# Where the taps of a depthwise convolution stand in VectorE's queue: behind each other, or one behind every eleventh matmul

## The chip, the cores and the metric

The kernel runs on one core of a Trainium2 chip. The metric is the device time of one execution in microseconds (us). The median of three runs of the kernel before is 1765.89 us (1764.24 to 1766.59). For this kernel, differences under about 0.2% (3.5 us) can't be told from no change.

## The reference, cut to what matters

One layer of a decoder trunk on 1024 tokens of 1024 channels. Three branches read the same normalized input and are merged by gates; a SwiGLU layer follows. The change touches branch B, the convolution module:

```python
a, ag = jnp.split(conv_in, 2, axis=-1)          # 512 channels each, from xn @ w_in
u = a * jax.nn.sigmoid(ag)
u = jnp.pad(u, ((0, 0), (30, 0), (0, 0)))
u = lax.conv_general_dilated(u, conv_w, (1,), 'VALID', ...,
                             feature_group_count=512) + conv_b   # depthwise, 31 taps, causal
u = jax.nn.silu(layer_norm(u, conv_ln_g, conv_ln_b))             # over the 512 channels
br_conv = u @ w_conv_out
```

Branch A is native sparse attention (compressed blocks, selected blocks, sliding window), branch C is cross-attention of 4 heads into 256 memory tokens. Everything is float32.

## The kernel before, in words

Every float32 product of two operands is made of three matmuls on halves that were split into a high and a low part (`mm3`, line 143, each through `mm`, line 140 and 141). The split is a copy on ScalarE (line 130) and a subtraction on VectorE or GpSimd (line 127, from `sub`).

The order of the instructions on each engine is not written by hand. The program is traced in the order of the source, and a planner then lays the instructions out when the program is built: it keeps a planned time for each engine and, where several instructions are ready, takes the one with the best priority, which is that of the source order. `with low(n)` makes the priority of what stands in it worse by n. What is in such a block is taken when nothing else is ready for the engine. On the chip each engine then runs its queue strictly in the planned order and waits at semaphores.

Two kinds of work have such a low priority. The **taps** (lines 356 to 361) are 31 VectorE instructions for each of four channel tiles `ct`, so 124: one `tensor_scalar` (line 358) and 30 `scalar_tensor_tensor` of about 1000 columns (line 360). The **fill** (lines 753 to 766) are 24 units of merge-gate projections into the bank `pf`, of which the first 12 (`N_EARLY`) may run whenever TensorE has nothing else; each unit is 48 matmuls of 512 columns, written out through ScalarE (`fz`, line 765).

The order of the source around the change is: memory query projection of two heads (`QMQ[0]`, 192 matmuls of `mm`), then for each `ct` the two GLU projections (96 matmuls of 512 columns for a `ct`, 24 for each of two halves and two weights) and the taps; the branch gates (32); the projections of the compressed keys and values (`compress_in`, 96) and their small network (`compress`, 36, with transposes and a VectorE copy at line 419 in between); the memory keys and values (`tok_proj`, 192); `mem_attention` twice (288 each: in four steps `tp`, 12 for scores, 48 of a projection, 12 for values); the last query projection `Q[1]` (192 in all). Then follows the layer norm of the convolution (lines 556 to 584): sums over the four channel tiles on GpSimd (`sum4`, line 560), a mean by a matmul with ones, squares, sums again, root, reciprocal, products, silu, and the store to `ud`. After it come the key and value projections KS, VS, KW, VW (lines 587 to 611) and the sparse attention.

A pool of 16 slabs holds the large tiles (`N_MAIN`): 8 of the normalized input, 4 of the convolution (`U`: input and accumulator of each `ct`, free after the store to `ud`), 2 of the queries, and others such as KS, VS, KW, VW.

The taps of the kernel before are traced inside the loop over `ct`, straight behind the GLU products of their own tile, and the planner lays each of them where VectorE has no other ready work.

Of the kernel before, what the change touches and what calls it, by code (L numbers as in the profile page):

```python
# [12 lines left out]
OP = mybir.AluOpType  # L13
# [5 lines left out]
S = 1024  # L19
# [10 lines left out]
TAPS = 31  # L30
FILL, TAP = 2000000, 1000000
ORDER = mybir.DependencyInfo(mybir.DependencyClass.NoSync, mybir.DependencyReason.DATA)
# [6 lines left out]
def hybrid_layer_kernel(  # L39
# [4 lines left out]
    nc = tc.nc  # L44
# [25 lines left out]
    def slab(shape, dt=F32R):  # L70
        return slabs.tile([P] + shape, dt, tag="slab", name=nm("slab"))
# [16 lines left out]
    def t2(shape, dt=F32, p=P):  # L88
        return t2p.tile([p] + shape, dt, tag="t2", name=nm("t2"))
# [8 lines left out]
    def bank(shape, dt=F32, p=P, at=None):  # L98
        if at is None:
            turn[1] += 1  # L100
            at = order[turn[1] % len(order)]
        return psp[at].tile([p] + shape, dt, tag=f"ps{at}", name=nm("ps"))
# [9 lines left out]
    def const(shape, dt, name, p=P):  # L112
        return cp.tile([p] + shape, dt, tag=name, name=name)
# [19 lines left out]
    def recip_rms(ss, n, eps, w):  # L133
# [3 lines left out]
        nc.vector.reciprocal(q, r)  # L137
        return q

    def mm(o, a, b, start, stop):  # L140
        return nc.tensor.matmul(o, a, b, start=start, stop=stop)  # L141

    def mm3(o, ah, al, bh, bl, start, stop):
        first = mm(o, ah, bh, start, False)
        mm(o, ah, bl, False, False)
        mm(o, al, bh, False, stop)
        return first
# [27 lines left out]
    cw = const([4, TAPS + 3], F32, "cw")  # L175
# [72 lines left out]
    def col_unit(w, c0, n=P, alloc=wslab, eng=None, load=False):  # L248
        return unit(w[:, c0:c0 + n].rearrange("(k p) c -> p k c", p=P), [w.shape[0] // P, n], alloc, eng,
                    load)  # L250
# [5 lines left out]
    def chan_proj(w, half, act=xn, n=P, alloc=bank):  # L256
        o = alloc([512])
        for k in range(KT):
            mm3(o[:n], w[:, 0, k, :], w[:, 1, k, :], act(0, k, half), act(1, k, half), k == 0, k == KT - 1)
        return o  # L260
# [28 lines left out]
    def head_norms(raw, gain):  # L289

        h, d = raw.shape[2:]
        ss = small(NT * h)
        for tp in range(4):
            sq = t2([2, h, d])
            nc.scalar.activation(sq, raw[:, 2 * tp:2 * tp + 2], AF.Square)
            nc.vector.tensor_reduce(ss[:, 2 * tp * h:2 * (tp + 1) * h], sq.rearrange("p a h d -> p (a h) d"),
                                    axis=AX.X, op=OP.add)
        r = recip_rms(ss, d, RMS_EPS, NT * h).rearrange("p (a h) -> p a h", a=NT)
        for tp in range(4):
            v = raw[:, 2 * tp:2 * tp + 2]  # L300
            nc.vector.tensor_tensor(v, v, r[:, 2 * tp:2 * tp + 2, :, None].to_broadcast([P, 2, h, d]), op=OP.mult)
            if gain is not None:
                gain_mul(v, gain)
# [27 lines left out]
    b = bank([4, TAPS + 3])  # L331
# [5 lines left out]
    b = bank([2, 16])  # L337
# [3 lines left out]
    nc.sync.dma_start(w2s, cmp_w2[0].rearrange("s (j p) d -> p s j d", p=P))  # L341


    U = []
    for ct in range(4):
        wag = col_unit(w_in, C_AG + ct * P)
        wa = col_unit(w_in, C_A + ct * P)
        uc = slab([2, S], F32)
        U.append(uc)
        for half in range(2):  # L350
            pg = chan_proj(wag, half)
            sg = t2([512])
            nc.scalar.activation(sg, pg, AF.Sigmoid)
            pa = chan_proj(wa, half)
            nc.vector.tensor_tensor(uc[:, 0, half * 512:(half + 1) * 512], pa, sg, op=OP.mult)
        with low(TAP):
            u, acc = uc[:, 0], uc[:, 1]
            nc.vector.tensor_scalar(acc, u, cw[:, ct, 30:31], cw[:, ct, 31:32], op0=OP.mult, op1=OP.add)
            for s in range(1, TAPS):
                nc.vector.scalar_tensor_tensor(acc[:, s:], u[:, :S - s], cw[:, ct, 30 - s:31 - s], acc[:, s:],  # L360
                                               op0=OP.mult, op1=OP.add)


    st = stage.tile([P, KT, 24], F32, tag="st", name=nm("st"))
# [14 lines left out]
    b = bank([NT, 24])  # L379
# [78 lines left out]
    for hp in range(2):  # L458
# [4 lines left out]
        b = bank([2, 256])  # L463
# [88 lines left out]
        raw_proj(ws, tp, Q[1])  # L552
    head_norms(Q[1], None)


    def sum4(part):
        for a, b_ in ((0, 1), (2, 3), (0, 2)):
            i0 = U[a][:, part] if (a, b_) != (0, 2) else U[0][:, 0]
            i1 = U[b_][:, part] if (a, b_) != (0, 2) else U[2][:, 0]
            nc.gpsimd.tensor_tensor(U[a][:, 0], i0, i1, op=OP.add)  # L560

    sum4(1)
    for half in range(2):
        c = slice(half * 512, (half + 1) * 512)
        pm_ = bank([512])
        mm(pm_, ones, U[0][:, 0, c], True, True)
        for ct in range(4):
            nc.vector.tensor_tensor(U[ct][:, 1, c], U[ct][:, 1, c], pm_, op=OP.subtract)
    for ct in range(4):
# [183 lines left out]
    with low(FILL):  # L753
        for n_ in range(3 * KT):
            b_, d_ = n_ // KT, n_ % KT
            w = col_unit(w_in, C_GM + b_ * D + d_ * P, alloc=fslab, eng=nc.gpsimd)
            for h_ in range(2):
                ps = fbank([512])
                for k in range(KT):
                    first = mm3(ps, w[:, 0, k, :], w[:, 1, k, :], xn(0, k, h_), xn(1, k, h_), k == 0, k == KT - 1)  # L760
                    j = ((n_ - N_EARLY) * 2 + h_) * KT + k
# [7 lines left out]
    acc = [slab([2, S], F32) for _ in range(4)]  # L769
# [3 lines left out]
    for n_, (br, src, wt) in enumerate(branches):  # L773
        ins = nxt
        for dp in range(4):
# [3 lines left out]
            for d_ in (2 * dp, 2 * dp + 1):  # L779
# [4 lines left out]
                for half in range(2):  # L784
# [7 lines left out]
                    a = acc[dp][:, d_ % 2, half * 512:(half + 1) * 512]  # L792
# [5 lines left out]
                    if n_ == 2:  # L798
                        if d_ % 2 == 0:
                            MG[half][dp] = slab([2, 2, 512])  # L800
                        m = MG[half][dp]
# [327 lines left out]
```

## Time and profile before

| | us |
|---|---|
| median of three runs | 1765.89 |
| lowest and highest run | 1764.24, 1766.59 |
| the profiled execution, whole | 1765.17 |
| its span, first to last instruction | 1763.4 |
| TensorE matmul busy in it | 1706.7 (97%) |
| VectorE busy in it | 1071.1 (61%) |
| ScalarE busy in it | 724.7 (41%) |
| GpSimd busy in it | 664.4 (38%) |

The trace calls the engines PE (TensorE matmul), PEld (its weight loads), DVE (VectorE), ACT (ScalarE), POOL (GpSimd) and SP (the queue of the transfers). In the tables of stretches a row begins with the stretch and its length; then each engine has its busy time in us and, in brackets, the number of its instructions that lie in the stretch; then come PEclk, the mean busy share of the transfer engines and what they moved in GB/s. PEclk is the granted clock of TensorE as a share of 2.4 GHz, so that 0.50 is the lower of its two levels, 1.2 GHz. In a timeline one row is a run of instructions of one kind, with its start, its length, the number merged into it, and in square brackets the idle time of the engine ahead of it and what ended that.

### The profile page before, as it was taken

To read this page: it belongs to the slowest core of one execution; us is meant where nothing else is said; L and a number is where in the kernel's file an instruction comes from. 1 tells how busy PE (TensorE), PEld (TensorE's weight loads), DVE (VectorE), ACT (ScalarE), POOL (GpSimd) and SP (SyncE) were. 2 spreads that over 40 slices of the span, in tenths; PEclk is the share of its full clock that TensorE was granted. 3 is DMA by queue.
4 is the path that set the end of the run, shared out by engine and by line. 5 is a ranking of instruction groups with operands and counts; after the bars stand their busy time and mean duration, and the time that the engine had idled before them with its cause. 6 is when DMAs were issued, how large, how long until landed. Compare 5 with 4: busy or idle time off the path is not lost.

```text
span 1763.4 us, 25092 instructions
## 1 busy us (share of the span) xinstructions
PE 1706.7 (97%) x9431; PEld 1482.2 (84%) x9431; DVE 1071.1 (61%) x1794; ACT 724.7 (41%) x1355; POOL 664.4 (38%) x543
## 2 busy tenths in 40 slices
PE   7999779999999999999999999989999999999999
PEld 6887669899988888989888899868888888888887
DVE  5599994435445667767755623596454554457655
ACT  6212224344455666766654423333222222234332
POOL 1113458333343434434203500456656767510000
PEclk9999899999999999999999999989999999999999
DMA  6113314211122111111286323123233444794673
GB/s 220 48 27 114 126 42 132 78 55 39 65 66 64 49 37 49 37 34 46 86 300 202 121 73 120 72 72 120 90 107 117 140 156 157 245 394 166 213 242 124
DMA packets 178527, 204.59 MB, mean 116 GB/s; under 512 B 10788, under 2 KB 125764, under 8 KB 177382
## 3 DMA queue, kind: packets, MB, share of 16 engines
q1 hardware_dynamic: 178406, 202.99, 35.2%
q8 instruction: 74, 1.21, 0.3%
q14 instruction: 47, 0.39, 0.1%
HBM read 152.62 MB, written 50.33 MB: 115 GB/s over the span
## 4 chain that ended last, share of the span: by engine, by line
PE 84%; DVE 10%; POOL 2%; ACT 1%; DMA 1%; issue 1%; SPq 0%; DVEq 0%; ACTq 0%; POOLq 0%
PE ps L141 51%; PE pf L141 16%; PE ps L1064 11%; DVE slab L360 6%; PE ps L714 3%; PE pf L1064 1%; DVE slab L127 1%; POOL wsl L127 1%; DVE t L127 1%; POOL t L127 1%; PE ps L208 1%; DMA slab<-in_x_dram 1%; DMA fst<-in_w_in_dram 0%; PE ps L640 0%; PE ps L515 0%
## 5 line engine op out<-in xcount | busy, mean ns | idle before, releaser
L141 PE MATMUL ps<-slab,wsl 128*128 128x512 f32 x1596 | 370.9, 390 | 0.3 <-ACT wsl L130 0.3
L141 PEld LDWEIGHTS ps<-slab,wsl 128*128 128x128 f32 x1596 | 299.0, 188 | 63.1 <-ACT wsl L130 0.8
L141 PE MATMUL pf<-slab,fsl 128*128 128x512 f32 x1260 | 327.8, 399 | 4.5 <-ACT fz L765 1.8
L141 PEld LDWEIGHTS pf<-slab,fsl 128*128 128x128 f32 x1260 | 226.6, 188 | 46.8 <-ACT fz L765 3.6
L141 PE MATMUL ps<-wsl,slab 128*128 128x256 f32 x1744 | 235.7, 291 | 12.9 <-POOL wsl L127 8.1
L141 PEld LDWEIGHTS ps<-wsl,slab 128*128 128x128 f32 x1744 | 225.3, 198 | 16.7 <-POOL wsl L127 8.5
L360 DVE SCALAR_TENSOR_TENSOR slab<-slab,cw 128x1007 f32<-128x1007 f32 (+27 forms) x120 | 174.5, 1501 | 0.4
L954 DVE TENSOR_TENSOR t<-ps,t 128x512 f32<-128x512 f32 x124 | 85.0, 688 | 109.2 <-PE ps L141 104.4
L127 DVE TENSOR_TENSOR t<-ps,t 128x512 fp32r<-128x512 f32 (+2 forms) x192 | 117.5, 630 | 44.6 <-ACT t L130 43.1
L141 PE MATMUL ps<-slab,fsl 128*128 128x512 f32 x612 | 142.1, 389 | 0.0
L141 PEld LDWEIGHTS ps<-slab,fsl 128*128 128x128 f32 x612 | 114.9, 188 | 23.9
L1064 PE MATMUL ps<-wsl 128*128 128x512 f32 x504 | 120.6, 389 | 0.0
L127 POOL TENSOR_TENSOR wsl<-st,wsl 128x1024 fp32r<-128x1024 f32 x20 | 72.9, 3659 | 122.9 <-ACT wsl L130 110.4
L141 PE MATMUL ps<-t,slab 128*128 128x256 f32 x624 | 115.6, 292 | 2.6 <-DVE t L127 2.1
L130 ACT CAST t<-ps 128x512 fp32r<-128x512 f32 (+2 forms) x192 | 97.9, 540 | 42.1 <-PE ps L714 30.5
L130 ACT CAST wsl<-st 128x1024 fp32r<-128x1024 f32 x66 | 69.3, 1050 | 110.5 <-PE ps L141 66.4
L1064 PEld LDWEIGHTS ps<-wsl 128*128 128x128 f32 x504 | 94.6, 188 | 19.6
L141 PEld LDWEIGHTS ps<-t,slab 128*128 128x128 f32 x624 | 93.9, 189 | 9.5 <-DVE t L127 3.0
L141 PE MATMUL ps<-slab,qt 128*128 128x384 f32 (+3 forms) x384 | 96.2, 342 | 0.5 <-DVE sm L682 0.5
L127 POOL TENSOR_TENSOR fsl<-fst,fsl 128x1024 fp32r<-128x1024 f32 x24 | 62.7, 2614 | 81.2 <-ACT fsl L130 81.2
L127 DVE TENSOR_TENSOR wsl<-st,wsl 128x1024 fp32r<-128x1024 f32 x46 | 62.3, 1355 | 49.9 <-ACT wsl L130 49.8
L628 POOL TENSOR_SCALAR wsl<-wsl,sm 128x640 f32<-128x640 f32 (+7 forms) x76 | 52.7, 707 | 91.2 <-DVE sm L626 53.4
(238 smaller groups left out, 2772.5 us busy)
## 6 DMA issues: line engine op xcount, KB each, us to landing
t<-in_w_down_dram SPq DMA_DIRECT2D x70, 256.0 KB, 3.8
fst<-in_w_in_dram SPq DMA_DIRECT2D x24, 512.0 KB, 3.9
zd<-fz SPq DMA_DIRECT2D x48, 256.0 KB, 2.0
t<-zd SPq DMA_DIRECT2D x24, 512.0 KB, 3.5
st<-in_w_in_dram SPq DMA_DIRECT2D x22, 512.0 KB, 3.9
st<-in_w_gate_dram SPq DMA_DIRECT2D x22, 512.0 KB, 4.0
st<-in_w_up_dram SPq DMA_DIRECT2D x22, 512.0 KB, 4.4
ad<-t SPq DMA_DIRECT2D x44, 256.0 KB, 2.4
```

The costliest lines, as they stand in the source:

```text
L127: eng.tensor_tensor(o, a, b, op=OP.subtract)
L130: nc.scalar.copy(hi, src)
L141: return nc.tensor.matmul(o, a, b, start=start, stop=stop)
L208: nc.tensor.transpose(b[:, kk, tt * P:(tt + 1) * P], js[tt][:, k * P:(k + 1) * P], ident)
L360: nc.vector.scalar_tensor_tensor(acc[:, s:], u[:, :S - s], cw[:, ct, 30 - s:31 - s], acc[:, s:], op0=OP.mult, op1=OP.add)
L628: nc.gpsimd.tensor_scalar(tiles[h], tiles[h], c[:, h:h + 1], 1.0, op0=OP.mult, op1=OP.mult)
L714: nc.tensor.transpose(b[:, j - j0, h, :], tiles[h][:, j * P:(j + 1) * P], ident)
L954: nc.vector.tensor_tensor(o, a_, b_, op=OP.add)
L1064: nc.tensor.matmul(B[t], a_, b_, start=start and k == 0 and j == 0, stop=k == FH - 1 and j == 2, skip_group_check=True)
```

## The change

A list `products` takes down every matmul that goes through `mm`, in the order of the source. The taps are no longer traced in the loop over `ct`: the loop only notes them, in the same order, and the place in `products` where the first tile's GLU products end. All 124 taps are traced after `head_norms(Q[1], None)`, ahead of the layer norm, with the same low priority as before. Tap `j` gets a manual dependency on one product: the products from the first place to the end of the `Q[1]` projection are divided into 128 equal parts, and tap `j` stands behind the first product of part `j`. The dependency is of the class `NoSync`: it holds for the planner's order and puts no semaphore into the program. The arithmetic of the taps is the same.

```diff
+    products = []
+
     def mm(o, a, b, start, stop):
-        return nc.tensor.matmul(o, a, b, start=start, stop=stop)
+        m = nc.tensor.matmul(o, a, b, start=start, stop=stop)
+        products.append(m.ins)
+        return m
...
-    U = []
+    U, taps, first_tap = [], [], None
+
+    def tap(ct, s):
+        u, acc = U[ct][:, 0], U[ct][:, 1]
+        if s == 0:
+            return nc.vector.tensor_scalar(acc, u, cw[:, ct, 30:31], cw[:, ct, 31:32], op0=OP.mult, op1=OP.add)
+        return nc.vector.scalar_tensor_tensor(acc[:, s:], u[:, :S - s], cw[:, ct, 30 - s:31 - s], acc[:, s:],
+                                              op0=OP.mult, op1=OP.add)
+
     for ct in range(4):
...
-        with low(TAP):
-            u, acc = uc[:, 0], uc[:, 1]
-            nc.vector.tensor_scalar(acc, u, cw[:, ct, 30:31], cw[:, ct, 31:32], op0=OP.mult, op1=OP.add)
-            for s in range(1, TAPS):
-                nc.vector.scalar_tensor_tensor(acc[:, s:], u[:, :S - s], cw[:, ct, 30 - s:31 - s], acc[:, s:],
-                                               op0=OP.mult, op1=OP.add)
+        taps += [(ct, s) for s in range(TAPS)]
+        first_tap = first_tap or len(products)
...
     head_norms(Q[1], None)
 
+
+    with low(TAP):
+        for j, (ct, s) in enumerate(taps):
+            at = first_tap + j * (len(products) - first_tap) // (len(taps) + 4)
+            tc.add_manual_dep(tap(ct, s).ins, products[at].name, ORDER, reason="taps along the projections")
```

## Rows read from the trace of the kernel before

**Rows 1.** The page: the span, busy time by engine, and TensorE in 40 slices.

```profile
span 1763.4 us, 25092 instructions
PE 1706.7 (97%) x9431; PEld 1482.2 (84%) x9431; DVE 1071.1 (61%) x1794; ACT 724.7 (41%) x1355; POOL 664.4 (38%) x543
...
PE   7999779999999999999999999989999999999999
```

**Rows 2.** Busy time by stretch: PE, PEld, DVE, ACT, POOL, then PEclk, DMA.

```profile
78.00:284.00 206.00, 182.37 (x873) 152.72 (x872) 195.12 (x164) 49.29 (x84) 85.38 (x25) 0.95 0.26 83
110.00:254.00 144.00, 128.48 (x597) 106.11 (x596) 143.94 (x117) 37.65 (x68) 57.37 (x18) 0.96 0.28 89
284.00:421.00 137.00, 136.32 (x1027) 130.24 (x1026) 52.10 (x86) 59.79 (x133) 51.36 (x50) 1.00 0.23 68
```

**Rows 3.** TensorE's longest waits, 100 to 300 us: total us, times, longest.

```profile
PE ps L141 <- DVE t L419: 9.6, 1, 9.6
PE ps L141 <- POOL wsl L127: 8.1, 1, 8.1
PE ps L141 <- DVE slab L127: 3.3, 2, 2.2
```

**Rows 4.** Timeline of VectorE and of TensorE around the longest wait.

```profile
172.42 31.51 DVE L360 SCALAR_TENSOR_TENSOR slab<-slab,cw 128x1005 f32<-128x1005 f32 x16
203.87 0.40 DVE L419 COPY t<-ps 128x256 f32<-128x256 f32 x1
...
188.13 0.38 PE L417 MATMUL ps<-ident,t 128*128 128x128 f32 x2
```

**Rows 5.** GpSimd's weight subtractions (line 127), 100 to 300 us: shortest, median, longest in ns.

```profile
L127 POOL TENSOR_TENSOR wsl<-st,wsl x13: 2367/3005/14845, 124.1 to 295.1; 128x1024 fp32r<-128x1024 f32 x13
```

**Rows 6.** Busy time by stretch, all engines, around the two long waits (columns of Rows 2).

```profile
200.00:205.00 5.00, 0.68 (x3) 0.68 (x4) 5.00 (x6) 0.00 (x0) 0.00 (x0) 0.50 0.39 107
205.00:210.00 5.00, 5.00 (x17) 4.39 (x17) 5.00 (x5) 4.08 (x9) 0.00 (x0) 0.66 0.00 0
265.00:270.00 5.00, 4.45 (x21) 4.45 (x22) 0.00 (x0) 0.00 (x0) 5.00 (x3) 0.51 0.48 155
```

**Rows 7.** The taps (line 360) by stretch: VectorE busy (x), clock, DMA share, GB/s.

```profile
78.00:110.00 32.00, 25.06 (x20) 1.00 0.15 36
110.00:254.00 144.00, 131.67 (x89) 0.96 0.28 89
142.00:188.00 46.00, 43.39 (x28) 1.00 0.50 166
78.00:284.00 206.00, 172.82 (x120) 0.95 0.26 83
284.00:421.00 137.00, 1.72 (x1) 1.00 0.23 68
```

**Rows 8.** All instructions of line 141 on TensorE, then those on `pf` alone, by stretch.

```profile
284.00:421.00 137.00, 130.43 (x935) 1.00 0.23 68
...
284.00:421.00 137.00, 32.42 (x130) 1.00 0.23 68
```

**Rows 9.** Timelines: GpSimd, TensorE in `mem_attention`; GpSimd, TensorE, VectorE near the layer norm.

```profile
304.10 1.84 POOL L505 TENSOR_SCALAR t<-t,sm 128x256 f32<-128x256 f32 x4 [2.36 <-DVE sm L501]
318.94 1.03 PE L515 MATMUL ps<-ident,t 128*128 128x128 f32 x8
...
287.94 4.89 POOL L560 TENSOR_TENSOR slab<-slab,slab 128x1024 f32<-128x1024 f32 x2
420.84 1.88 PE L141 MATMUL ps<-slab,ones 128*128 128x512 f32 x4
469.56 0.43 DVE L127 TENSOR_TENSOR slab<-ps,slab 128x256 fp32r<-128x256 f32 x1 [0.44 <-ACT slab L130]
```

**Rows 10.** The stores of the convolution (line 584): issue, and time to landing.

```profile
L584 SPq DMA_DIRECT2D ud<-slab x4: 319/320/320, 448.6 to 452.4; - x4
...
DMA to landing us min/median/max: 2.7/3.4/4.6
```

## The prediction

> **What bounds the kernel now.** I read the page first. TensorE's matmuls are busy for 1706.7 us of the 1763.4 us span, and the least full of its slices are the first, the fifth and the sixth [rows 1]. So nearly all of this kernel is bound by TensorE, and a change on VectorE can only give back time where TensorE stands still or runs at its lower clock. The fifth and sixth slices are 176 to 264 us, and there the taps run. Next I read the engines by stretch. From 110 to 254 us VectorE is busy for 143.94 of 144 us while TensorE is busy for 128.48; from 284 to 421 us, where the memory attention and the last query projection are, TensorE is busy for 136.32 of 137 us and VectorE for only 52.10 [rows 2]. So VectorE's taps are packed into a stretch that they fill, and the stretch behind it is nearly free of them: 1.72 us of 174.5 [rows 7].
>
> Then the waits. From 100 to 300 us TensorE waited 9.6 us for the copy at line 419, 8.1 us for a weight subtraction on GpSimd, and 3.3 us for split halves from VectorE: 21.0 us in three places [rows 3]. TensorE's whole idle time from 78 to 284 us is 206.00 - 182.37 = 23.6 us [rows 2], so 2.6 us are left for small waits. The timeline shows how the longest comes about. The transposes that the copy reads end at 188.5 us; the copy runs at 203.87, behind 16 taps that take 31.51 us; that is 15.4 us after what it reads is there [rows 4]. The second is the other engine's side of the same thing: one GpSimd subtraction that takes 2.37 us at its shortest took 14.85 us while VectorE ran taps without a break [rows 5].
>
> The waits also cost clock. From 200 to 205 us and from 265 to 270 us, at the end of the two long waits, the granted clock is 0.50 and 0.51, that is the 1.2 GHz level, and 0.66 on average from 205 to 210 [rows 6]. Busy time times the missing share gives 0.68 x 0.50 + 5.00 x 0.34 + 4.45 x 0.49 = 0.3 + 1.7 + 2.2 = 4.2 us of lost work.
>
> **What is removed.** The taps stay 124 and their sum stays; what moves is their place. By the source, `products` has 192 + 96 = 288 entries when the first tile's GLU products end, and 288 + 288 + 32 + 96 + 36 + 192 + 576 + 192 = 1700 after `Q[1]`. So 1412 products are divided by 128, and there is one tap to 11.03 products; the last one, j = 123, stands at product 1644. I place product numbers in time by counting back from 421 us: 935 matmuls of line 141 less 130 of fill are 805 products from 284 to 421 us [rows 8], so product 895 is at 284 us, and 805 / 11.03 = 73 less the 5 unused parts at the end leave 68 taps there. 56 stay ahead of 284 us.
>
> In the stretch from 78 to 284 us VectorE then has 195.12 - 172.82 = 22.3 us of other work [rows 2, 7] and 56 taps, which at 172.82 / 120 = 1.44 us [rows 7] make 80.6 us: 103 of 206 us, or of the 181 us that are left if the stretch shrinks by what follows. VectorE is then half free, an instruction like the copy of line 419 stands behind one tap and not behind 16, and GpSimd finds gaps. So I take away the three waits that end in VectorE or in the starved GpSimd, 9.6 + 8.1 + 3.3 = 21.0 us, and the 4.2 us of clock, and leave the 2.6 us of small waits: **25.2 us removed**. The bounds are 9.6 + 2.0 = 11.6 us (the copy's wait alone, with the clock of 200 to 210 us) and 23.6 + 4.2 = 27.8 us.
>
> **What is added.** The same 68 taps now stand from 284 to 421 us, where they meet the softmax of the memory attention. VectorE's other work there is 52.10 - 1.72 = 50.4 us [rows 2, 7]. What a tap costs there the trace doesn't show, so it is bounded: 25.06 / 20 = 1.25 us in a stretch where GpSimd has nothing to do, and 43.39 / 28 = 1.55 us beside a busy GpSimd; from 110 to 254 us, with GpSimd busy for 40% of the stretch, it is 131.67 / 89 = 1.48 us [rows 2, 7]. From 284 to 421 us GpSimd is busy for 51.36 of 137 us, 37% [rows 2], so 1.48 us is the nearest row. The demand is 50.4 + 68 x 1.48 = 151.0 us in 137 us: a backlog of 14.0 us. With 1.25 us it is 135.4 us and none; with 1.55 us it is 155.8 us, a backlog of 18.8 us.
>
> How much of a backlog TensorE feels depends on who waits. The softmax is a step ahead: its last GpSimd products end at 305.94 us and the transposes that read them start at 318.94 [rows 9], 13 us later, which hides it. The halves of the transposed probabilities, though, stand straight between two groups of matmuls, and so do the score tiles of the next step; cover there is the fill, 130 matmuls in 32.42 us of the stretch [rows 8]. I take half of the backlog, **7 us added**, between 0 and 18.8. A single tap that happens to be running holds up a waiting instruction for 1.48 us at most; TensorE's fill hides that, and without it two such places in each of 8 steps would cost up to 24 us, which is inside the last rival.
>
> **The layer norm comes later.** Now the adds of tiles 2 and 3 and of both pairs are done at 292.8 us, and the mean's matmul is issued at 420.84 behind the projection [rows 9]. After the change they can't start before the last tap, near the end of the projection, and take 4.89 us. So the layer norm moves by 4.9 us plus the backlog, by 5 to 24 us and by 12 to 19 at what I take. Behind it the slabs of `U` come free when the stores land, now at 452.4 + 3.4 = 455.8 us [rows 10]; with 8 + 4 + 2 slabs taken, KS and VS fit, and KW and VW need those slabs. The first write to VW is at 469.56 us [rows 9], so 13.7 us of delay are free and 0 to 10 us come beyond it. I cost this at nothing, hidden by the fill that TensorE has left; if the fill has run out by then, it costs up to 10 us.
>
> The edge itself puts no wait into the program, and nothing of SP's queue is moved. The planner's other choices may shift, which I can't size.
>
> **The sum.** The profiled execution: 1763.4 - 25.2 + 7.0 = 1745.2 us of span, and 1.8 us around it as before, 1747.0; the median of the runs lies 0.7 us above that execution, so 1747.7, rounded to 1748 us, 1.0% faster. The backlog's bounds alone give 1741 to 1760.
>
> **A rule against it.** The profile's row shows one GpSimd subtraction of 14.85 us beside unbroken taps [rows 5], and 16 taps of 1.97 us each beside GpSimd's adds [rows 4]. The Trainium skill, page "SBUF — State Buffer", section "Who interferes with whom", says that a VectorE instruction with two SBUF inputs, as a tap has, contends with a GpSimd instruction that reads SBUF, and that the second to issue blocks until the first has ended. By that rule a GpSimd instruction would lose one tap's time and then run, some 4 us and not 14.85, so the measurement is worse than the rule; and each GpSimd instruction from 284 to 421 us would now meet taps that it doesn't meet today. That speaks for the last rival below.
>
> **The rivals.**
> First, **all of it comes off**: taps at 1.25 us leave no backlog and the small waits go too, 1765.9 - 27.8 = 1738 us. For it speaks that TensorE loses only 0.7 us from 284 to 421 us today; against it that 135.4 of 137 us leaves no room for one collision.
> Second, **the change doesn't do what it says**: the edge orders plans, not the chip. If the planner lets several taps wait for a free VectorE and then lays them in bunches ahead of an instruction that the chip needs sooner, GpSimd is starved as now, and only the copy's wait goes: 1765.9 - 11.6 = 1754 us at best, 1766 at worst. For it speaks that the 16 taps ahead of the copy were the plan's own choice; against it, that 11 products of 512 columns now lie between two taps.
> Third, on the other side, **VectorE becomes the bound of the memory attention**. One mechanism: taps and GpSimd's instructions lengthen each other where TensorE waits for both in every step. It pays for the whole gain when the backlog reaches 25.2 us, at a tap of (137 + 25.2 - 50.4) / 68 = 1.64 us, and shows as slower from 1.70 us. The 16 taps from 172 us, beside a GpSimd without a pause, took 31.51 / 16 = 1.97 us [rows 4]; at that the backlog is 47.4 us and the time 1788. Half way between, at 1.83 us, it is 37.8 us and **1778 us**. For it speaks that the demand is above the stretch even at 1.48; against it, that GpSimd has pauses there and that a free VectorE ahead of 284 us can't run into debt first.
>
> **How the numbers follow.** The forecast has 0.58, the first rival 0.08, the second 0.14 (half of it within 0.2%), the third 0.20 (a tenth of it within 0.2%, the rest slower). Faster: 0.58 + 0.08 + 0.07 = 0.73; same: 0.07 + 0.02 = 0.09; slower 0.18. About 0.2%, 3.5 us, is what a measurement of this kernel can tell from no change. The range goes from the first rival's 1738 us past the second to 1768, where the third starts to show; what lies outside is most of the third.
>
> **What would show it.** Right: the wait for line 419 and the long subtraction are gone, the granted clock stays at 1.00 from 180 to 280 us, taps run until about 421 us, VectorE is near half busy before the memory attention and near full in it. Wrong: waits of TensorE for lines 127, 494 or 527 on VectorE or for line 505 on GpSimd inside the memory attention, taps of 1.7 us or more there, a wait at the mean's matmul, or a wait for KW and VW behind the stores to `ud`.

## The result, and the profile after

The changed kernel takes 1755.91 us (median of six runs, 1754.58 to 1756.79) where the kernel before, on the same chip in the same session, takes 1766.04 us: a ratio of 0.9945, 95% interval 0.9932 to 0.9958, so 10.1 us faster. The forecast was 1748 us, 18 us faster, and it gave 1741 to 1760 us for its own case.

The page of the profiled execution (compare [rows 1]; the columns are the same):

```profile
span 1754.7 us, 25091 instructions
...
PE 1709.4 (97%) x9431; PEld 1484.7 (85%) x9431; DVE 1080.2 (62%) x1794; ACT 723.6 (41%) x1355; POOL 655.1 (37%) x543
...
PE   7999999999999999999999999989999999999999
```

The fifth and sixth slices are at nine tenths or more now. The span is 8.7 us shorter (the 10.1 us above are the difference of the medians). That is made of two terms with different signs: TensorE's idle time falls from 1763.4 - 1706.7 = 56.7 to 1754.7 - 1709.4 = 45.3 us, by 11.4 us, and its busy time rises by 2.7 us although its matmuls are the same. Where the idle time went is seen by stretch (columns as in [rows 2], whose first and third row are answered by the first two rows here; the third row is the whole part of the kernel in which taps and their layer norm run):

```profile
78.00:284.00 206.00, 199.38 (x1087) 173.32 (x1086) 153.91 (x137) 63.87 (x121) 76.61 (x37) 0.99 0.29 91
284.00:421.00 137.00, 130.64 (x875) 119.36 (x874) 118.05 (x128) 52.13 (x105) 59.35 (x41) 0.98 0.20 62
60.00:560.00 500.00, 486.13 (x2920) 430.40 (x2919) 340.39 (x484) 184.41 (x410) 199.21 (x155) 0.99 0.23 73
```

From 78 to 284 us TensorE's idle time falls from 23.6 to 6.6 us; from 284 to 421 us it rises from 0.7 to 6.4 us. VectorE is no longer full over the whole of the first stretch, and is busy for 118 of 137 us behind. But the halves hide where it is full now: from 205 to 300 us, in the memory keys and the first steps of the memory attention, it is busy for 92 of 95 us.

```profile
205.00:300.00 95.00, 88.84 (x636) 83.61 (x636) 92.42 (x83) 39.16 (x81) 57.53 (x31) 0.98 0.26 81
```

What TensorE waits for from 60 to 560 us, the changed kernel (total us, times, longest; compare [rows 3]):

```profile
PE ps L143 <- DVE t L127: 4.7, 2, 2.4
PE pf L143 <- ACT fz L778: 2.9, 5, 0.7
PE ps L474 <- POOL t L290: 2.4, 1, 2.4
PE ps L143 <- POOL slab L573: 1.9, 1, 1.9
PE ps L143 <- DVE slab L127: 1.4, 1, 1.4
```

The third row is a transpose of the memory keys behind their products with the gain on GpSimd (line 290), and these wait for the norm of the keys on VectorE, which stands behind five taps. The wait for the copy (now line 427) and the one for the starved subtraction are gone. The subtractions of the weights (line 127 on GpSimd, 60 to 300 us) now take 2.38 to 3.42 us, where one took 14.85 us [rows 5]:

```profile
L127 POOL TENSOR_TENSOR wsl<-st,wsl x15: 2380/2974/3424, 125.7 to 298.0; 128x1024 fp32r<-128x1024 f32 x15
```

In their place stand short waits, of which the largest are for the halves of the transposed probabilities in the memory attention (`t`, line 127 on VectorE). VectorE's timeline at the second of them (start, length, what ran):

```profile
360.44 7.91 DVE L354 SCALAR_TENSOR_TENSOR slab<-slab,cw 128x1012 f32<-128x1012 f32 x3
368.28 0.68 DVE L535 COPY t<-ps 128x512 f32<-128x512 f32 x1
368.88 1.25 DVE L354 SCALAR_TENSOR_TENSOR slab<-slab,cw 128x1009 f32<-128x1009 f32 x1
370.06 1.27 DVE L127 TENSOR_TENSOR t<-ps,t 128x512 fp32r<-128x512 f32 x2
```

GpSimd's timeline over the same stretch:

```profile
360.55 3.42 POOL L127 TENSOR_TENSOR wsl<-st,wsl 128x1024 fp32r<-128x1024 f32 x1
363.92 3.37 POOL L127 TENSOR_TENSOR fsl<-fst,fsl 128x1024 fp32r<-128x1024 f32 x1
```

VectorE's timeline at the first wait:

```profile
265.83 6.93 DVE L354 SCALAR_TENSOR_TENSOR slab<-slab,cw 128x1021 f32<-128x1021 f32 x5
272.69 1.27 DVE L127 TENSOR_TENSOR t<-ps,t 128x512 fp32r<-128x512 f32 x2
```

And TensorE's timeline at all three places, the idle time before a row and what ended it in brackets:

```profile
273.42 1.83 PE L143 MATMUL ps<-t,slab 128*128 128x256 f32 x11 [2.28 <-DVE t L127]
370.79 1.01 PE L143 MATMUL ps<-t,slab 128*128 128x256 f32 x3 [2.42 <-DVE t L127]
410.61 2.83 PE L143 MATMUL ps<-slab,ones 128*128 128x512 f32 x4 [1.87 <-POOL slab L573]
```

Three taps that meet two GpSimd subtractions take 7.91 us, 2.6 us each, and the copy, one more tap and the split stand behind them. The first wait is behind five taps in a row. The third is the mean's matmul of the layer norm, which waits for the adds behind the last tap.

Behind each of these three waits TensorE runs at the lower of its clock levels for a while. Busy time by stretch, all engines:

```profile
25.00:30.00 5.00, 5.00 (x15) 3.97 (x16) 4.41 (x6) 3.72 (x8) 0.12 (x1) 0.66 0.77 207
275.00:280.00 5.00, 5.00 (x31) 5.00 (x31) 4.98 (x7) 1.68 (x7) 0.00 (x0) 0.66 0.05 19
370.00:375.00 5.00, 4.21 (x23) 4.21 (x24) 4.93 (x6) 2.52 (x5) 0.00 (x0) 0.66 0.54 149
410.00:415.00 5.00, 4.39 (x9) 2.50 (x10) 3.23 (x6) 0.36 (x2) 2.86 (x2) 0.66 0.32 88
```

A granted clock of 0.66 over 5 us is 3.4 us at 1.2 GHz, in nearly all of which TensorE was busy, so about 1.7 us of work lost at each, 5.1 us behind the three waits. Before, the two long waits cost 4.2 us [rows 6]. The first row lies 50 us ahead of the first tap and is not of the change; the kernel before has nearly the same idle time ahead of it (2.35 us from 20 to 25 us, 2.40 in the changed kernel) and keeps its clock:

```profile
25.00:30.00 5.00, 4.78 (x21) 3.97 (x22) 4.54 (x6) 3.91 (x9) 0.17 (x1) 1.00 0.76 194
```

The 1.7 us of the first row and the 0.9 us between 5.1 and 4.2 make 2.6 of the 2.7 us by which busy time rises.

### The profile page after: what moved, and what is told of

Same layout as the page of the kernel before. It is cut to its first block, busy times and chain, and to the rows that moved or that the text cites. A ratio compares the mean times of both kernels' runs of the same rounds, so it can differ in the third digit from the quotient of the medians.

```text
span 1754.7 us, 25091 instructions
## 1 busy us (share of the span) xinstructions
PE 1709.4 (97%) x9431; PEld 1484.7 (85%) x9431; DVE 1080.2 (62%) x1794; ACT 723.6 (41%) x1355; POOL 655.1 (37%) x543
## 4 chain that ended last, share of the span: by engine, by line
PE 87%; DVE 6%; POOL 2%; ACT 2%; DMA 1%; issue 1%; SPq 0%; DVEq 0%; POOLq 0%; ACTq 0%
PE ps L143 53%; PE pf L143 17%; PE ps L1077 11%; PE ps L727 3%; DVE slab L354 3%; PE pf L1077 1%; DVE t L127 1%; DVE slab L127 1%; POOL t L127 1%; PE ps L212 1%; DMA slab<-in_x_dram 1%; DMA fst<-in_w_in_dram 0%; PE ps L653 0%; PE ps L711 0%; POOL wsl L127 0%
## 5 line engine op out<-in xcount | busy, mean ns | idle before, releaser
L354 DVE SCALAR_TENSOR_TENSOR slab<-slab,cw 128x1023 f32<-128x1023 f32 (+15 forms) x120 | 188.1, 1568 | 2.0
L127 POOL TENSOR_TENSOR wsl<-st,wsl 128x1024 fp32r<-128x1024 f32 x20 | 57.7, 2895 | 130.0 <-ACT wsl L130 124.6
L130 ACT CAST wsl<-t 128x1024 fp32r<-128x1024 f32 x43 | 45.3, 1054 | 92.6 <-POOL t L127 39.0
```

The lines of the kernel that those rows point to most:

```text
L127: eng.tensor_tensor(o, a, b, op=OP.subtract)
L130: nc.scalar.copy(hi, src)
L354: return nc.vector.scalar_tensor_tensor(acc[:, s:], u[:, :S - s], cw[:, ct, 30 - s:31 - s], acc[:, s:], op0=OP.mult, op1=OP.add)
```

## The experiments

The time of each kernel and its ratio to runs of the kernel before on the same chip; the number in the last column is the mean of one tap (of the 120 `scalar_tensor_tensor`) in the profiled execution; in the kernel before it is 1.501.

| kernel | median us | before, us | ratio (95%) | tap, us |
|---|---|---|---|---|
| the change | 1755.91 | 1766.04 | 0.9945 (0.9932 to 0.9958) | 1.568 |
| no edge | 1765.60 | 1766.32 | 0.9996 (0.9987 to 1.0006) | 1.570 |
| no taps | 1737.50 | 1766.32 | 0.9839 (0.9823 to 0.9856) | |
| bunches of 16 | 1761.43 | 1766.32 | 0.9976 (0.9966 to 0.9986) | 1.586 |
| spaced by columns | 1741.25 | 1766.32 | 0.9861 (0.9846 to 0.9875) | 1.438 |
| ended early | 1756.61 | 1764.40 | 0.9949 (0.9935 to 0.9964) | 1.597 |
| softmax products on ScalarE | 1753.37 | 1764.40 | 0.9931 (0.9915 to 0.9948) | 1.532 |
| columns, products on ScalarE | 1741.44 | 1764.40 | 0.9862 (0.9848 to 0.9877) | 1.435 |
| columns, ended early | 1748.58 | 1764.40 | 0.9903 (0.9889 to 0.9918) | 1.478 |
| GpSimd relieved by ScalarE | 1754.90 | 1765.21 | 0.9948 (0.9930 to 0.9966) | 1.338 |
| kernel before, relieved so | 1756.93 | 1765.21 | 0.9956 (0.9941 to 0.9971) | 1.355 |
| GpSimd writes zeros | 1751.44 | 1765.89 | 0.9916 (0.9900 to 0.9933) | 1.374 |
| columns, GpSimd writes zeros | 1742.45 | 1765.89 | 0.9870 (0.9855 to 0.9884) | 1.323 |

**The later place without the edge.** The taps are traced where the change traces them, and stand behind no product:

```diff
-            at = first_tap + j * (len(products) - first_tap) // (len(taps) + 4)
-            tc.add_manual_dep(tap(ct, s).ins, products[at].name, ORDER, reason="taps along the projections")
+            tap(ct, s)
```

> The changed kernel with the taps traced at the same late place, but without the edge to a product. Theory of pace (the edge holds taps back, so that VectorE's queue stays short ahead of what TensorE waits for): with no edge the planner packs the taps as before, the 9 us waits for the copy and for a starved GpSimd subtraction come back, 1763 to 1768 us. Rival, place (it is the later place in the source that changes the plan): same as the changed kernel, 1754 to 1758 us.

Measured 1765.60 us, ratio 0.9996: no change. Its VectorE timeline has the row of [rows 4] again, the copy behind 16 taps:

```profile
172.89 31.51 DVE L354 SCALAR_TENSOR_TENSOR slab<-slab,cw 128x1005 f32<-128x1005 f32 x16
204.33 0.40 DVE L427 COPY t<-ps 128x256 f32<-128x256 f32 x1
```

The later place alone does nothing; the gain needs the edge. (An edge with the taps traced at their old place was not run.) The two long waits did not both come back, though: TensorE waits 9.7 us for the copy, but 2.6 us and not 8.1 for a subtraction on GpSimd, of which the longest takes 9.89 us. Its idle time from 60 to 560 us is 20.3 us where the kernel before has 25.2, and some 3 us more are lost to the clock there.

**The floor.** The kernel before with 30 of 31 taps left out:

```diff
-            for s in range(1, TAPS):
-                nc.vector.scalar_tensor_tensor(acc[:, s:], u[:, :S - s], cw[:, ct, 30 - s:31 - s], acc[:, s:],
-                                               op0=OP.mult, op1=OP.add)
```

> The kernel before with 30 of the 31 taps of each channel tile left out, so that the convolution is one product with one weight; nothing else changes. It is the floor for any placing of the taps. Theory of pace: the changed kernel still pays for taps that collide with GpSimd in the memory attention and for a late layer norm, so the floor lies well below it, 1737 to 1746 us. Rival, the rest lies elsewhere: the taps cost nothing any more after the change, 1752 to 1757 us.

Measured 1737.50 us. The taps cost the kernel before 28 to 29 us and the changed kernel still 18.4 us, so about a third of their cost was removed. The prediction's bound for what could come off, 27.8 us, was the right size.

**Bunches.** The same rate, 16 taps behind every 176th product. The end, which the expectation below calls the same, is earlier: the last bunch stands behind product 1523, and the last tap of the change behind 1644.

```diff
-            at = first_tap + j * (len(products) - first_tap) // (len(taps) + 4)
+            at = first_tap + j // 16 * 16 * (len(products) - first_tap) // (len(taps) + 4)
```

> The changed kernel with 16 taps behind every 176th product in place of one behind every eleventh: same average rate, same end, but in bunches. Theory of pace: a bunch can stand ahead of a copy again and gives GpSimd no gap, so part of the gain goes, 1759 to 1765 us. Rival, rate alone matters and not one by one: 1754 to 1758 us.

Measured 1761.43 us, ratio 0.9976: the gain is halved. TensorE's waits from 60 to 300 us show a split behind taps (3.2 us) and GpSimd's softmax products (2.9 us):

```profile
PE ps L143 <- DVE slab L127: 3.2, 1, 3.2
PE ps L523 <- POOL t L513: 2.9, 2, 2.3
```

So the later stretch alone does not give the gain, and an even pace counts as well; a part of the difference can lie in the earlier end. No subtraction of the weights was starved in this run: from 60 to 300 us the longest takes 3.38 us.

**Spaced by columns.** A product counts by its moving columns, 512 or 256, in place of by one:

```diff
+        widths.append(512 if b.shape[-1] > 256 else 256)
...
-            at = first_tap + j * (len(products) - first_tap) // (len(taps) + 4)
+            want = sum(widths[first_tap:]) * j // (len(taps) + 4)
+            at, run = first_tap, 0
+            while run < want:
+                run += widths[at]
+                at += 1
```

> The changed kernel with the taps spaced by the moving columns of the products (512 or 256) in place of by their number: about 20 more taps beside the products of 512 columns, fewer in the memory attention. Theory of pace with a collision in the memory attention: fewer taps meet the softmax and GpSimd there, 1746 to 1752 us. Rival, what is left doesn't hang on the density there: 1754 to 1758 us.

Measured 1741.25 us, ratio 0.9861 (0.9846 to 0.9875): better than both theories had it, 25 us below the kernel before, 14.7 us below the changed one and 3.8 us above the floor. By stretch:

```profile
78.00:284.00 206.00, 205.54 (x1159) 180.44 (x1158) 167.87 (x159) 68.47 (x134) 79.82 (x41) 1.00 0.29 90
284.00:421.00 137.00, 133.47 (x906) 121.96 (x905) 96.40 (x111) 50.47 (x99) 58.38 (x44) 1.00 0.20 62
60.00:560.00 500.00, 494.56 (x3008) 439.66 (x3008) 336.07 (x520) 194.33 (x438) 198.61 (x167) 1.00 0.24 75
```

All that TensorE waits for from 60 to 560 us:

```profile
PE pf L143 <- ACT fz L783: 4.9, 5, 1.5
PE ps L658 <- POOL t L654: 0.2, 1, 0.2
PE ps L143 <- DVE sm L700: 0.2, 1, 0.2
```

No wait for a tap is left, the granted clock is 1.00 in all three rows, and TensorE's idle time from 60 to 560 us is 5.4 us where the changed kernel has 13.9. VectorE works more ahead of 284 us (167.87 against 153.91 us) and less behind (96.40 against 118.05). From 205 to 300 us, where the changed kernel has it busy for 92.42 of 95 us, it has air now:

```profile
205.00:300.00 95.00, 93.48 (x666) 87.83 (x666) 75.10 (x83) 43.64 (x86) 55.16 (x31) 1.00 0.33 101
```

**Ended early.** The changed kernel's spacing by number, drawn together so that the last tap stands at product 1445:

```diff
-            at = first_tap + j * (len(products) - first_tap) // (len(taps) + 4)
+            at = first_tap + j * (len(products) - first_tap) // (len(taps) + 26)
```

> The changed kernel with the taps spread over the first 124 of 150 equal parts of the products in place of 128, so that the last one stands at product 1446, in the second memory attention, and not at 1644. Theory of the late layer norm (what is left is the wait at the mean's matmul and the clock behind it, 1.9 + 1.7 us): 1750 to 1753 us. Rival, density in the memory attention (one tap to 9.4 products is denser there, more collisions): 1754 to 1760 us.

Measured 1756.61 us, ratio 0.9949 against 0.9945. The wait at the mean is gone, but from 60 to 300 us TensorE now waits longer for GpSimd's gain products and for a split:

```profile
PE ps L474 <- POOL t L290: 3.2, 1, 3.2
PE ps L143 <- DVE slab L127: 1.9, 1, 1.9
```

In the memory attention it waits up to 3.3 us for a split, and the clock falls in three short stretches again, at 225, 245 and 300 us. The theory of the late layer norm, taken alone, falls. The same with the spacing by columns (124 of 140 parts):

> Taps spaced by columns, over the first 124 of 140 parts in place of 128, so that they end earlier and the layer norm with them, at a density that is 9% higher. Late layer norm: 1738 to 1741 us. Density: 1742 to 1748 us.

Measured 1748.58 us, 7 us slower than the spacing by columns at 128 parts. From 60 to 300 us TensorE now has waits that the wider spacing does not have, 4.8 us in all, for the norm of the memory tokens on VectorE, the gain products and the copy:

```profile
PE ps L213 <- DVE slab L204: 2.6, 2, 1.9
PE ps L475 <- POOL t L291: 1.7, 1, 1.7
PE ps L143 <- DVE t L428: 0.5, 1, 0.5
```

Another 1.7 us of work are lost to the clock at 465 us, behind a wait of 2.40 us for the drain of the fill, which is not of the density. So here a density that is 9% higher costs more than an earlier layer norm gives, but not all of the 7 us is the density's.

**Softmax products on ScalarE.** The collision theory at the place where the prediction had put it:

```diff
-                nc.gpsimd.tensor_scalar(pm[:, tt, h, :], pm[:, tt, h, :], rec[:, j:j + 1], 1.0,
-                                        op0=OP.mult, op1=OP.mult)
+                nc.scalar.activation(pm[:, tt, h, :], pm[:, tt, h, :], AF.Copy, scale=rec[:, j:j + 1])
```

> The changed kernel with the softmax products of the memory attention (32 instructions of line 513) on ScalarE in place of GpSimd; the taps stay where they are. Theory of collision (taps and GpSimd's instructions lengthen each other in the memory attention, and TensorE waits there for VectorE): the waits at the split of the transposed probabilities shrink, 1745 to 1751 us. Rival, density alone (VectorE is too full there whoever its neighbour is): 1753 to 1758 us.

Measured 1753.37 us, ratio 0.9931, whose interval overlaps that of the change: 2.5 us by the ratios, and perhaps nothing. TensorE waits 4.7 us for the splits of the probabilities as before, and its idle time from 60 to 560 us is 13.3 us against 13.9; what is less in the profiled execution is the lost clock, one stretch of 1.7 us there in place of three. The same edit with the spacing by columns:

> Taps spaced by columns, and the softmax products of the memory attention on ScalarE. Theory of collision: a part of the 3.8 us between the spacing by columns and the kernel without taps goes, 1738 to 1741 us. Rival, what is left there is the late layer norm and the drain of the fill: 1741 to 1743 us.

Measured 1741.44 us, ratio 0.9862 against 0.9861: nothing. So no cost of the taps' meeting these products can be told from nothing.

**GpSimd relieved by ScalarE.** The low halves that GpSimd would subtract are left out and ScalarE writes a copy; the softmax products are on ScalarE too:

```diff
     def split(hi, lo, src, eng=None):
         nc.scalar.copy(hi, src)
+        if eng is nc.gpsimd and free[0]:
+            nc.scalar.copy(lo, src)
+            return
...
```

> The changed kernel with GpSimd relieved up to the last query projection: the low halves of the weights that GpSimd subtracts there, and those of the first 12 fill units, are left out (ScalarE writes a plain copy in their place), and the softmax products of the memory attention run on ScalarE. The taps stay where they are. Theory of collision (the taps are long because they meet GpSimd's reads): taps fall from a mean of 1.57 us to about 1.3 us, and most of the 18 us between the changed kernel and the one without taps goes, 1738 to 1746 us. Rival, density alone: taps fall but TensorE goes on waiting for VectorE, 1748 to 1756 us.

Measured 1754.90 us. The taps shorten from 1.57 to 1.34 us as the collision theory has it, and the waits for VectorE and GpSimd nearly vanish; but new waits for ScalarE, which got the work, take their place (first rows of TensorE's waits from 60 to 560 us):

```profile
PE pf L148 <- ACT fz L784: 5.9, 5, 2.4
PE ps L148 <- ACT t L132: 4.2, 1, 4.2
PE ps L148 <- POOL slab L577: 0.8, 1, 0.8
```

As a test of the time this run is spoiled by its own edit. The same edit in the kernel before:

> The kernel before with the same relief of GpSimd (low halves of those weights left out, softmax products on ScalarE). Theory of collision: taps fall from 1.45 us to about 1.25 us, the 8.1 us wait for the starved subtraction goes with its clock, the copy behind 16 taps waits less but still waits: 1748 to 1758 us. Rival, the backlog is the planner's own and not GpSimd's: 1760 to 1767 us.

Measured 1756.93 us: a relief of GpSimd gives the kernel before 8 us, nearly as much as the change does, with 14 taps still ahead of the copy. TensorE's wait for that copy is 0.4 us where it was 9.6: the copy runs 7.1 us after its transposes where it was 15.4, and 27 matmuls of the fill cover nearly all of that. So a queue of taps costs only what TensorE has no other work for.

```profile
174.93 24.96 DVE L365 SCALAR_TENSOR_TENSOR slab<-slab,cw 128x1019 f32<-128x1019 f32 x14
199.82 0.41 DVE L424 COPY t<-ps 128x256 f32<-128x256 f32 x1
```

**GpSimd writes zeros.** The cleaner form: the subtractions are left out, and GpSimd writes zeros in their place, which reads nothing and gives ScalarE no work:

```diff
     def split(hi, lo, src, eng=None):
         nc.scalar.copy(hi, src)
+        if eng is nc.gpsimd and blank[0]:
+            nc.gpsimd.memset(lo.bitcast(F32), 0.0)
+            return
...
```

> The changed kernel with the low halves of the weights that GpSimd subtracts up to the last query projection, and of the first 12 fill units, left out: GpSimd writes zeros in their place, an instruction that reads nothing. ScalarE gets nothing more to do and the softmax products stay on GpSimd. Theory of collision (a tap and a GpSimd subtraction of 1024 columns block each other): the waits for VectorE's splits and for GpSimd go and nothing takes their place, 1740 to 1748 us. Rival, density alone: 1751 to 1756 us.

Measured 1751.44 us, ratio 0.9916 against 0.9945, on the edge of both theories: about 5 us, and the two intervals just touch (0.9933 and 0.9932). The taps fall to 1.374 us, VectorE is busy for 81.2 of 95 us from 205 to 300 us, and TensorE waits from 60 to 560 us for no split and no gain product any more (the first two rows of its waits; the third is 0.2 us):

```profile
PE pf L148 <- ACT fz L785: 4.9, 5, 2.4
PE ps L148 <- POOL slab L578: 1.9, 1, 1.9
```

What is left beside the drain of the fill is the layer norm's wait. But the profiled execution has four short stretches at the lower clock ahead of 700 us, at 41, 396, 478 and 655 us; only that at 396 is behind a wait that hangs on the taps. That at 478 follows the wait of 2.40 us for the drain of the fill (first row above), that at 655 lies at two waits of 1.34 and 0.31 us in the sparse attention, and that at 41 lies ahead of the first tap. With the spacing by columns:

> Taps spaced by columns, and GpSimd's subtractions up to the last query projection and of the first 12 fill units left out in the same way. Theory of collision: little is left to gain where the taps already miss the subtractions that matter, 1737 to 1741 us; if it comes below the kernel without taps (1737.5 us), the lost subtractions themselves are worth something and the other run has to be read less that much. Rival, density alone: as the spacing by columns by itself, 1740 to 1743 us.

Measured 1742.45 us, ratio 0.9870, as without the zeros (0.9861), though the taps fall from 1.438 to 1.323 us. Where the taps are spaced by columns, no cost of the subtractions that they meet can be told from nothing.

## Why the prediction came out as it did

**The cause was right.** The edge and not the later place alone holds the taps back; the wait for line 419 and the starved subtraction are gone; of TensorE's idle time from 78 to 284 us 17.0 us came off, where the prediction took 21.0. The time moved the way that was forecast, by a little more than half of what was forecast.

**Where the taps stand was misplaced.** The prediction put 68 taps from 284 to 421 us by the old timeline. The changed kernel has fewer there:

```profile
78.00:284.00 206.00, 113.14 (x73) 0.99 0.29 91
284.00:421.00 137.00, 74.91 (x47) 0.98 0.20 62
```

(taps alone, as in [rows 7]). The places in the source are the ones that were worked out, but the plan moved under them: the first transposes of the values step, at 306.3 us before, are at 265.6 us. Of these 41 us some 19 are idle time that is gone, some 19 are fill that is no longer laid ahead of them (31.5 us on `pf` from 78 us to these transposes against 50.1; from 284 to 421 us it is 48.66 against 32.42, [rows 8]), and the rest is clock. The memory attention came earlier and met the same taps earlier. So the backlog was costed in the wrong stretch: the idle time that was added lies from 224 to 411 us.

The load was also misjudged by counting products. The prediction has "11 products of 512 columns" between two taps; by the source only 416 of the 1412 products have 512 columns, and the other 996, from the small network of the compressed keys on, have 256 or fewer. The changed kernel's timeline of TensorE shows what each kind takes:

```profile
255.60 10.12 PE L143 MATMUL ps<-wsl,slab 128*128 128x256 f32 x83
403.00 5.74 PE L143 MATMUL pf<-slab,fsl 128*128 128x512 f32 x24 [0.67 <-ACT fz L778]
```

That is 0.122 us and 0.239 us for one. So by estimate eleven products of 512 columns give VectorE 2.6 us for a tap, and eleven of 256 only 1.35 us, with no fill in between: less than a tap took there, and VectorE has other work too. That fits where VectorE is full, from 205 us on. Spaced by columns, a tap has 14.3 products of 256, 1.74 us by the same estimate, and VectorE is not full.

**The price of a tap was too low.** It was taken at 1.48 us, between 1.25 and 1.55. From 284 to 421 us it is 74.91 / 47 = 1.59 us, and from 205 to 300 us 67.98 / 41 = 1.66 us (taps alone below), both above the upper bound:

```profile
205.00:300.00 95.00, 67.98 (x41) 0.98 0.26 81
```

The upper bound came from 142 to 188 us of the kernel before, called a stretch beside a busy GpSimd; GpSimd is busy there for 21.5 of 46 us. The 1.97 us of the last rival, too, was not beside a GpSimd without a pause: over those 16 taps it is busy for 20.8 of 32 us. The spacing by itself does not make the taps dearer: the mean of one is 1.50 us before, 1.57 with the edge and 1.57 without it. Taking the subtractions away does make them cheaper (1.374 us).

**The waits that were added came out near their size, by luck.** 7 us was taken as half of a backlog in the stretch from 284 to 421 us; the idle time there rose by 5.7 us. But VectorE is not over its time there (118.05 of 137 us), of the 5.7 us only 2.42 are a wait for VectorE, and 1.87 belong to the layer norm. The other waits behind taps lie ahead of 284 us, 2.44 (the gain products), 1.43 and 2.28 us of the 6.6 us that stay. The place that the prediction named, the halves of the transposed probabilities, is the largest of them in sum.

**The clock is the term that failed.** 4.2 us were booked as given back because the two long waits would go. They did go, and 5.1 us came in behind three waits of 1.87 to 2.42 us. The prediction had no clock price for the waits that it added. Set against its sum of 25.2 - 7.0 = 18.2 us, the two profiled executions differ by 17.0 us of idle time ahead of 284 us in place of 21.0, less 5.7 us of idle time behind in place of 7.0, less 0.9 us of clock in place of a gain of 4.2, less the 1.7 us of clock at 25 us that is not of the change: 8.7 us, which is the difference of their spans. The largest miss is the clock's, 5.1 us; the next is the 4.0 us of idle time that stay ahead of 284 us.

**The layer norm** cost a wait of 1.87 us and its clock, where the prediction had hidden it. Its last tap is at 404.4 us and not at 421. Ending it early (1756.61 us) did not pay, because the taps then are denser.

**The rivals.** That all of it comes off was not reached by the change, but by the spacing by columns to within 4 us. That the change doesn't do what it says falls, since both long waits are gone and without the edge there is no gain; in small it is seen, where the plan lays five taps in a row ahead of a split. That VectorE becomes the bound of the memory attention is what happened in small, and it began ahead of it: VectorE is full from 205 to 300 us. Its price of 1.64 us for a tap, at which the whole gain would have gone, was worked out for 68 taps in a stretch that has 47, so the measured 1.59 us can't be held against it. The Trainium skill, page "SBUF — State Buffer", section "Who interferes with whom", has a tap contend with a GpSimd instruction that reads and not with one that only writes. The runs agree: with GpSimd writing zeros in place of subtracting, the tap falls from 1.568 to 1.374 us, and the zeros take 0.95 to 0.98 us each, also those beside taps.

**What stays open.** Of the 18.4 us that the taps still cost the changed kernel, 14.7 us go by a spacing that puts about 20 more of them beside the products of 512 columns, and about 5 us by taking away the subtractions that they meet. In the profiled executions the first number is 8.5 us of idle time (13.9 to 5.4 us from 60 to 560 us), 5.1 us of clock behind the three waits and the 1.7 us at 25 us. In both runs VectorE is less full from 205 to 300 us (75.1 and 81.2 us against 92.4); how much is that fullness and how much is the planner's other order isn't told apart, since every run with another spacing has another plan on all engines.

## What to carry to other kernels

Filler work for an engine that runs its queue in order can be paced by an edge to the work that it should hide behind, and in this kernel the pace did best when it followed the length of that work and not its count: one tap to a fixed number of columns gave 25 us, one to a fixed number of matmuls 10, and bunches of 16 five. When a stall is moved, its price is the wait and, often, the clock behind it: three of the four waits of 1.9 to 2.4 us cost nearly as much in clock as one of 9. Places worked out on the old timeline shift when the planner has free fill to move, so a forecast should count the load by instruction order and by the length of the instructions, not by old time.

## What the runs showed of the hardware that was not expected

TensorE's clock fell to 1.2 GHz behind idle times as short as 1.87 to 2.42 us, each time at a cost of 1.7 us of work, nearly as much as the wait; the two waits of 8.1 and 9.6 us before cost 2.2 and 2.0 us [rows 6]. Not every such wait has a price: that for the gain products, 2.44 us up to 224.7 us in the same execution, has none behind it. Busy time of all engines behind it, with the granted clock at 1.00:

```profile
225.00:230.00 5.00, 5.00 (x40) 4.78 (x39) 4.86 (x6) 3.96 (x6) 2.84 (x1) 1.00 0.02 5
230.00:235.00 5.00, 5.00 (x29) 4.35 (x28) 4.96 (x5) 0.00 (x0) 5.00 (x3) 1.00 0.33 106
```

What tells the one kind from the other stays open.

Who pays when VectorE and GpSimd meet is not settled either. In the kernel before a GpSimd subtraction took 14.85 us beside taps without a gap [rows 5], while the 16 taps without a gap from 172 us were themselves stretched to 1.97 us each [rows 4], beside GpSimd instructions of at most 3.5 us. With the edge no subtraction of the weights took more than 3.42 us; without it, with the taps packed again, the longest took 9.89 us. So unbroken taps can starve a GpSimd instruction, and do not always.
